# A decoder layer on one core: low parts of the projections' weights by an adding transfer in place of a subtraction

## The chip, the cores and the metric

The kernel runs on one core of a Trainium2 chip. The core has five engines that run their own instruction lists side by side: TensorE (PE, matmuls, with its weight loads as PEld), VectorE (DVE), ScalarE (ACT), GpSimd (POOL) and SyncE (SP, which here only issues transfers). Transfers between the chip's memory and the core's own memory run on 16 transfer engines; SyncE, ScalarE and GpSimd can issue them. The metric is the device time of one execution in microseconds; times are given as the median of some runs.

## What is computed

One layer with two token mixers, a merge, and a feed-forward part, in float32, for 512 tokens of width 1024:

```python
proj = x @ w_in                                     # 1024 x 8720, the projections
q, k, v, z, b_raw, a_raw, lru_x, lru_g, gate_dn, gate_lru = split(proj)
qkv  = silu(causal_depthwise_conv([q, k, v], dn_conv_w))
o    = gated_delta_rule_chunked(l2(q), l2(k), v, g, beta)
y_dn = (rms(o) * dn_norm_w * silu(z)) @ w_branch_dn
h    = rg_lru(causal_depthwise_conv(lru_x, lru_conv_w) + lru_conv_b, ...)
y_lru = (h * gelu(lru_g)) @ w_branch_lru
merged = sigmoid(gate_dn + b) * y_dn + sigmoid(gate_lru + b) * y_lru
h = layer_norm(alpha * x + merged @ w_out)
h = layer_norm(alpha * h + (silu(h @ w_gate) * (h @ w_up)) @ w_down)
```

## The kernel before

Every large product is made of three matmuls in a reduced float32 format: both operands are split into a high part, rounded to that format, and a low part, the remainder. `mm3` (line 154) issues high x high, high x low and low x high (lines 155, 156, 157), so line 157 is the one that reads the low part of the weights.

A weight block is 128 columns of a matrix: a tile of 128 partitions by 8 row groups by 128 columns, 512 KB, read in rows of 512 bytes. `load_w` (line 164) has SyncE fetch it into `wr` (3 buffers). `split_w` (line 173) makes the high part `wh` and the low part `wl` (3 buffers each, pool `wp`): `split_flat` (line 133) has ScalarE round the block into `wh` (line 135) and then subtracts `wh` from `wr` into `wl` (line 121), on VectorE in one piece or, where it is told `G`, on GpSimd in two halves of 512 columns.

`columns` (line 404) turns a matrix's columns into jobs of one block: fetch and split, then 8 x 3 matmuls of 512 tokens into one PSUM bank, then a function that takes the result on (conv, gate, SiLU). `play` (line 303) keeps the block in work and two more fetched ahead. All projections (`dn_proj`, `z_proj`, `lru_pair`, `gate_pair`) run through `columns` with `G`, in an order written in line 20: 64 blocks, called block 0 to block 63 here in the order in which TensorE works on them, from about 43 to 509 us. Between the steps of a block `advance` lets small chains onto TensorE: the delta rule of each head pair (`dn_chain`) and the gates of each LRU pair (`lru_chain`), whose other work lies on VectorE, ScalarE and GpSimd (masks, copies, clears). TensorE's list is ordered by hand from a table of latencies (line 23); the other engines' lists are ordered by a scheduler at build time, each engine then runs its list strictly in order.

The first FFN pair (line 1090) is split ahead of its use into tiles `f0h` and `f0l` of its own, also with `G`: four blocks. The branch matrices, `w_out` and the rest of the FFN are split with VectorE's subtraction; the change leaves them as they are.

Of the kernel before, what the change touches and what calls it, by code (L numbers as in the profile page):

```python
# [11 lines left out]
AF = mybir.ActivationFunctionType  # L12
ALU = mybir.AluOpType
# [20 lines left out]
P = 128  # L34
T = 512
D = 1024
NK = D // P
# [4 lines left out]
CQ, CK, CV, CZ, CB, CA = 0, 1024, 2048, 3072, 4096, 4104  # L42
# [4 lines left out]
def layer_kernel(  # L47
# [9 lines left out]
    V, S, G, PE = nc.vector, nc.scalar, nc.gpsimd, nc.tensor  # L57
# [13 lines left out]
    def slot(name, dt=F32):  # L71
        if not line:
            raise RuntimeError(f"no slot for {name}")
        tag = line.pop(0)
        t = big.tile([P, 2, T], dt, tag=tag, name=name)
        held[id(t)] = (t, tag)
        return t
# [12 lines left out]
    def bankp(name):  # L90
        return bank("p", name)
# [4 lines left out]
    def urgent():  # L96

        return tc.high_priority(offset=500)
# [12 lines left out]
    def f(ap):  # L111
        return ap.bitcast(F32)

    def flat(t):
        return t.rearrange("p a b -> p (a b)")
# [4 lines left out]
    def tt(eng, o, a, b, op):  # L120
        return eng.tensor_tensor(out=o, in0=a, in1=b, op=op)  # L121
# [4 lines left out]
    def act(o, i, func, **kw):  # L126
        return S.activation(out=o, in_=i, func=func, **kw)  # L127
# [5 lines left out]
    def split_flat(hi, lo, src, eng=None):  # L133

        S.copy(out=hi, in_=src)  # L135
        n = src.shape[1]
        step = 512 if eng is G else n
        for c in range(0, n, step):
            tt(eng or V, lo[:, c:c + step], src[:, c:c + step], f(hi[:, c:c + step]), ALU.subtract)
# [14 lines left out]
    def mm3(ps, wh, wl, rh, rl, start, stop):  # L154
        PE.matmul(ps, wh, rh, start=start, stop=False)  # L155
        PE.matmul(ps, wh, rl, start=False, stop=False)  # L156
        PE.matmul(ps, wl, rh, start=False, stop=stop)  # L157
# [3 lines left out]
    def view_w(t, a, b):  # L161
        return t[:, :a * b].rearrange("p (a b) -> p a b", a=a)

    def load_w(src, raw=None):

        wcount[0] += 1
        if raw is None:
            raw = wp.tile([P, 1024], F32, tag="wr", bufs=3, name=f"wr{wcount[0]}")
        v = view_w(raw, *src.shape[1:])
        nc.sync.dma_start(out=v, in_=src)  # L170
        return v

    def split_w(raw, eng=None, hi=None, lo=None):

        wcount[0] += 1
        if hi is None:
            hi = wp.tile([P, 1024], F32R, tag="wh", name=f"wh{wcount[0]}")
        if lo is None:
            lo = wp.tile([P, 1024], F32R, tag="wl", name=f"wl{wcount[0]}")
        n = raw.shape[1] * raw.shape[2]  # L180
        split_flat(hi[:, :n], lo[:, :n], raw.rearrange("p a b -> p (a b)"), eng)
        return view_w(hi, *raw.shape[1:]), view_w(lo, *raw.shape[1:])

    def rows(w):
        return w.rearrange("(kt p) c -> p kt c", p=P)

    win = rows(w_in[0])
# [51 lines left out]
    xT = []  # L239
# [23 lines left out]
    with tc.manual_schedule(engines={mybir.EngineType.Activation, mybir.EngineType.DVE}):  # L263
        for k in range(NK):
            transpose_x(k)
            if k == 1:
                n = NK * 16
# [22 lines left out]
    def advance(flush=False):  # L290
        while flush and chains:
            clock[0] += 0.68
            advance()
        for ch in list(chains):
            while ch in chains and ch[0] <= clock[0]:
                try:
                    pe, lat = next(ch[1])
                    ch[0] = clock[0] + pe + lat
                    clock[0] += pe
                except StopIteration:  # L300
                    chains.remove(ch)
# [19 lines left out]
    def start(gen, lat):  # L321
        chains.append([clock[0] + lat, gen])
# [71 lines left out]
    for b in range(4):  # L394
        G.tensor_copy(out=eye32[32 * b:32 * b + 32],
                      in_=ident[32 * b:32 * b + 32, 32 * b:32 * b + 32])
# [4 lines left out]
    V.tensor_reduce(out=up, in_=eye32[:, 0:16], axis=AX.X, op=ALU.add)  # L401
    V.tensor_reduce(out=low, in_=eye32[:, 16:32], axis=AX.X, op=ALU.add)

    def columns(src, rhs, name, then, eng=None, nk=NK):

        def job(j):
            def fetch():
                return split_w(load_w(src[:, :, j * P:j * P + P]), eng)

            def use(wh, wl):  # L410
                ps = bankp(f"{name}_{j}")
                for k in range(nk):
                    mm3(ps, wh[:, k], wl[:, k], rhs[k][:, 0], rhs[k][:, 1], k == 0, k == nk - 1)
                    if k < nk - 1:
                        yield
                then(j, ps)
                yield
            return fetch, use

        for j in range(src.shape[2] // P):  # L420
            yield job(j)

    def conv(o, ps, w, n, **kw):
        with urgent():
            act(o, ps, AF.Identity, scale=w(3, n), **kw)
            for d in (1, 2, 3):
                stt(o[:, d:], ps[:, :T - d], w(3 - d, n), o[:, d:], ALU.mult, ALU.add)
# [15 lines left out]
    def dn_proj(col, p):  # L443
        t = qkv[col, p] = slot(f"x{col}_{p}")

        def then(j, ps):
            conv(t[:, j], ps, qkv_w, col // P + 2 * p + j)
            act(t[:, j], t[:, j], AF.Silu)
            if j == 1:
                done[f"{col}_{p}"] = clock[0] + LAT["conv"]  # L450

        if col == CK:
            start(dn_chain(p), 0.0)
        if p == 0 and col != CV:
            for j in range(2):
                then(j, first[(0 if col == CK else 2) + j])
        else:
            c = col + 256 * p
            yield from columns(win[:, :, c:c + 256], xT, f"pj{col}_{p}", then, G)

    sz = [None] * 4

    def z_proj(p):
        sz[p] = slot(f"sz{p}")

        def then(j, ps):
            with urgent():
                act(sz[p][:, j], ps, AF.Silu)
            if j == 1:
                done[f"{CZ}_{p}"] = clock[0]  # L470

        c = CZ + 256 * p
        yield from columns(win[:, :, c:c + 256], xT, f"pj{CZ}_{p}", then, G)

    def dn_chain(p):

# [295 lines left out]
    def lru_pair(p):  # L772
        n0 = 2 * p
        u, r, ig = slot(f"u{p}"), slot(f"r{p}"), slot(f"ig{p}")
        gw = wg.tile([P, 4, P], F32, tag="gr" if p % 2 else "gs", name=f"gr{p}")
        nc.sync.dma_start(out=gw[:, 0:2], in_=lru_w_a[0, n0:n0 + 2].rearrange("n i o -> i n o"))
        nc.sync.dma_start(out=gw[:, 2:4], in_=lru_w_i[0, n0:n0 + 2].rearrange("n i o -> i n o"))

        def then_u(j, ps):
            conv(u[:, j], ps, lru_w, n0 + j, bias=lru_p(0, n0 + j))  # L780
            if j == 1:
                start(lru_chain(p, u, r, ig, gw), LAT["u"])

        keep = []

        def then_g(j, ps):
            keep.append(ps)
            if j == 1:
                while p not in gls:
                    clock[0] += 0.68  # L790
                    advance()
                with urgent():
                    for i in range(2):
                        act(gls[p][:, i], keep[i], AF.Gelu_apprx_tanh)
                done[f"gl{p}"] = clock[0]

        c = CLX + 256 * p
        yield from columns(win[:, :, c:c + 256], xT, f"lx{p}", then_u, G)
        c = CLG + 256 * p
        yield from columns(win[:, :, c:c + 256], xT, f"lg{p}", then_g, G)  # L800

    def lru_chain(p, u, r, ig, gw):
        n0 = 2 * p
# [33 lines left out]
    def gate_pair(col, p):  # L837
        g = slot(f"g{col}_{p}")

        def then(j, ps):  # L840
            with urgent():
                act(g[:, j], ps, AF.Sigmoid, bias=gate_b((0 if col == CGD else 8) + 2 * p + j))

        c = col + 256 * p
        yield from columns(win[:, :, c:c + 256], xT, f"g{col}_{p}", then, G)
        gates[p + (0 if col == CGD else 4)] = g

    def before_merge():
# [22 lines left out]
    for n in range(4 * NK):  # L871
# [7 lines left out]
        wh, wl = [t.rearrange("p (j k c) -> p j k c", j=2, k=2) for t in ws[k // 2]]  # L879
# [144 lines left out]
    for i in range(4):  # L1024
        t = slot(f"h1{i}")
# [16 lines left out]
    for m in range(4):  # L1042
        wh, wl = split_w(load_w(wo[:, 2 * m:2 * m + 2, 0:512]))
        for i in range(4):
            ts = slice(i * P, (i + 1) * P)
            for k in (2 * m, 2 * m + 1):
                mm3(pss[i], mT[k][:, 0, ts], mT[k][:, 1, ts], wh[:, k % 2], wl[:, k % 2], k == 0, k == NK - 1)
# [6 lines left out]
    for i in range(4):  # L1054
        ps = bankp(f"mx1_{i}")
        ts = slice(i * P, (i + 1) * P)
        for k in range(NK):
            if i > 1 and k == (5 if i == 2 else 3):
                transpose_h(i - 2)
            wh, wl = ws[k // 2]  # L1060
# [29 lines left out]
    for n, (src, then) in enumerate(ffn_pair(0)):  # L1090
        for j in range(2):
            tiles = [slot(f"f0{m}{n}{j}", F32R) for m in "hl"]
            wh, wl = split_w(load_w(src[:, :, j * P:j * P + P]), G, *[flat(t) for t in tiles])
            work.append((bankp(f"f0{n}{j}"), wh, wl, then, j, tiles))
    for half in range(2):
        ts = slice(256 * half, 256 * half + 256)
# [20 lines left out]
    for j in range(2):  # L1117
# [5 lines left out]
        for m in range(NF // 2):  # L1123
# [4 lines left out]
            for i in range(4):  # L1128
                ts = slice(i * P, (i + 1) * P)
                last = m == NF // 2 - 1  # L1130
                for c, ps in tops[i]:
                    n = ps.shape[1]
# [35 lines left out]
```

## Time and profile before

| | |
|---|---|
| median of 3 runs | 1030.63 us (1030.3 to 1031.08) |
| the profiled execution | 1029.83 us, of which the span of the profile is 1028.1 |
| TensorE busy | 999.7 us (97%), mean granted clock 0.995 |
| VectorE, ScalarE, GpSimd busy | 545.1, 425.5, 247.6 us |
| subtractions on GpSimd for the projections | 128, 172.4 us together |
| roundings of blocks on ScalarE | 145, 151.8 us together |
| transfers issued by SyncE for blocks of the projections | 64 of 512 KB, 3.7 us to land in the median |

A share of busy time is an average over stages; what a change is worth is read from the stage where it lies. In the rows, "wl<-wr,wh" is an operation that writes `wl` from `wr` and `wh`; the numbers of single buffers are left out. Rows of the timeline begin with the start (us from the span's start) and the duration (us), and end with the idle time of the engine ahead of the row and what ended it. A transfer's "issue" row is its time on the engine that issues it; "to landing" runs from issue to the landing of its data.

### The profile page before, as it was taken

What the parts mean: (1) busy time and instruction counts of PE and PEld (TensorE: products, weight loads), DVE (VectorE), ACT (ScalarE), POOL (GpSimd) and SP (SyncE); (2) the same over time, 40 slices, a digit from 0 to 9 for tenths busy, and PEclk for the clock granted to TensorE, in tenths of its full rate; (3) what the DMA queues carried; (4) which work ended last, traced back from release to release, by engine and by line L of the source; (5) the groups of instructions that cost most, each with busy time, mean ns of one, the idle gap of its engine ahead of it and who ended that gap; (6) DMA issues with size and microseconds to landing.
All of it is one profiled execution on the core that took longest, in us unless ns stands there. A gap on an engine that the chain in (4) does not pass through costs nothing. (4 is left out here: it accounts for less than half of the span.)

```text
span 1028.1 us, 14179 instructions
## 1 busy us (share of the span) xinstructions
PE 999.7 (97%) x5630; PEld 824.5 (80%) x5630; DVE 545.1 (53%) x1161; ACT 425.5 (41%) x576; POOL 247.6 (24%) x234
## 2 busy tenths in 40 slices
PE   7999989999999999999999999999999999999995
PEld 4887767877887888788888888898888888888885
DVE  3769989837777872264333556823333333312426
ACT  5589463368326643764321333323223322321222
POOL 2372624516332723274100003000000000000006
PEclk9999999999999999999999999999999999999998
DMA  8332223223222323154334337003333433333222
GB/s 252 106 101 54 80 73 84 63 72 82 63 62 73 87 63 93 47 142 115 102 94 153 103 115 213 1 23 101 103 95 110 123 103 88 97 103 100 85 62 82
DMA packets 150663, 96.79 MB, mean 94 GB/s; under 512 B 4476, under 2 KB 139837, under 8 KB 150597
## 3 DMA queue, kind: packets, MB, share of 16 engines
q1 hardware_dynamic: 148064, 91.52, 30.8%
q0 software_dynamic: 1216, 4.20, 1.2%
q8 instruction: 44, 0.72, 0.3%
q10 hardware_dynamic: 1316, 0.16, 0.1%
q14 instruction: 23, 0.18, 0.1%
HBM read 93.76 MB, written 2.11 MB: 93 GB/s over the span
## 5 line engine op out<-in xcount | busy, mean ns | idle before, releaser
L135 ACT CAST wh<-wr 128x1024 fp32r<-128x1024 f32 x145 | 151.8, 1048 | 410.5 <-issue 132.8
L121 POOL TENSOR_TENSOR wl<-wr,wh 128x512 fp32r<-128x512 f32 x128 | 172.4, 1369 | 216.5 <-ACT wh L135 207.0
L121 DVE TENSOR_TENSOR wl<-wr,wh 128x1024 fp32r<-128x1024 f32 x81 | 99.2, 1225 | 206.8 <-ACT wh L135 206.8
L155 PE MATMUL pj<-xT,wh 128*128 128x512 f32 x224 | 92.5, 413 | 0.0
L156 PE MATMUL pj<-xT,wh 128*128 128x512 f32 x224 | 88.2, 394 | 0.0
L157 PE MATMUL pj<-xT,wl 128*128 128x512 f32 x224 | 88.2, 394 | 0.0
L127 ACT ACT_TABLE_LOAD x62 | 79.5, 1283 | 12.3 <-DMA rw<-in_lru_conv_w 6.8
L156 PE MATMUL dn<-wl,fT 128*128 128x512 f32 (+1 forms) x168 | 63.3, 377 | 0.0
L155 PE MATMUL dn<-wh,fT 128*128 128x512 f32 (+1 forms) x168 | 63.3, 377 | 0.0
L157 PE MATMUL dn<-wh,fT 128*128 128x512 f32 (+1 forms) x168 | 63.2, 376 | 0.0
L156 PE MATMUL fg<-hk,wh 128*128 128x512 f32 x160 | 62.3, 389 | 0.0
L155 PE MATMUL fg<-hk,wh 128*128 128x512 f32 x160 | 62.3, 389 | 0.0
L157 PE MATMUL fg<-hk,wl 128*128 128x512 f32 x160 | 62.2, 389 | 0.0
L155 PE MATMUL fu<-hk,wh 128*128 128x512 f32 x160 | 62.2, 389 | 0.0
L156 PE MATMUL fu<-hk,wh 128*128 128x512 f32 x160 | 62.2, 389 | 0.0
L157 PE MATMUL fu<-hk,wl 128*128 128x512 f32 x160 | 62.2, 389 | 0.0
L121 POOL TENSOR_TENSOR h<-h,g 128x512 f32<-128x512 f32 x6 | 8.1, 1358 | 193.2 <-ACT h L127 193.2
L155 PE MATMUL g<-xT,wh 128*128 128x512 f32 x128 | 51.1, 399 | 0.0
L157 PE MATMUL g<-xT,wl 128*128 128x512 f32 x128 | 50.0, 391 | 0.0
L157 PEld LDWEIGHTS pj<-xT,wl 128*128 128x128 f32 x224 | 42.5, 190 | 9.3
L156 PE MATMUL g<-xT,wh 128*128 128x512 f32 x128 | 49.9, 390 | 0.0
L124 DVE SCALAR_TENSOR_TENSOR x<-pj,cols,x 128x511 f32<-128x511 f32 (+2 forms) x60 | 44.5, 742 | 9.9 <-ACT x L127 9.5
(358 smaller groups left out, 2241.6 us busy)
## 6 DMA issues: line engine op xcount, KB each, us to landing
wr<-in_w_in SPq DMA_DIRECT2D x64, 512.0 KB, 3.7
wr<-in_w_ffn_gate SPq DMA_DIRECT2D x22, 512.0 KB, 3.7
wr<-in_w_ffn_up SPq DMA_DIRECT2D x22, 512.0 KB, 3.6
wr<-in_w_ffn_down SPq DMA_DIRECT2D x22, 512.0 KB, 3.7
wr<-in_w_branch_lru SPq DMA_DIRECT2D x8, 512.0 KB, 3.6
wr<-in_w_branch_dn SPq DMA_DIRECT2D x8, 512.0 KB, 4.0
wr<-in_w_out SPq DMA_DIRECT2D x8, 512.0 KB, 4.2
wk<-in_w_in SPq DMA_DIRECT2D x8, 256.0 KB, 6.1
```

What stands on the lines that cost most here:

```text
L121: return eng.tensor_tensor(out=o, in0=a, in1=b, op=op)
L124: return V.scalar_tensor_tensor(out=o, in0=a, scalar=s, in1=b, op0=op0, op1=op1)
L127: return S.activation(out=o, in_=i, func=func, **kw)
L135: S.copy(out=hi, in_=src)
L155: PE.matmul(ps, wh, rh, start=start, stop=False)
L156: PE.matmul(ps, wh, rl, start=False, stop=False)
L157: PE.matmul(ps, wl, rh, start=False, stop=stop)
```

## The change

For the projections and the first FFN pair the low part is no longer subtracted by GpSimd. ScalarE writes the negated block into `wl` (rounded to the same format as the high part), and GpSimd issues a second transfer of the same block from the chip's memory, which adds what it reads to what lies in `wl`. ScalarE also rounds the block into `wh`, as before. The fetch into `wr` by SyncE stays.

```diff
-    def split_w(raw, eng=None, hi=None, lo=None):
+    def split_w(raw, src=None, hi=None, lo=None):
...
-        split_flat(hi[:, :n], lo[:, :n], raw.rearrange("p a b -> p (a b)"), eng)
-        return view_w(hi, *raw.shape[1:]), view_w(lo, *raw.shape[1:])
+        flat_raw = raw.rearrange("p a b -> p (a b)")
+        h, l = view_w(hi, *raw.shape[1:]), view_w(lo, *raw.shape[1:])
+        if src is None:
+            split_flat(hi[:, :n], lo[:, :n], flat_raw)
+        else:
+            act(lo[:, :n], flat_raw, AF.Copy, scale=-1.0)
+            G.dma_start(out=l, in_=src, accum_op=ALU.add)
+            S.copy(out=hi[:, :n], in_=flat_raw)
+        return h, l
...
-    def columns(src, rhs, name, then, eng=None, nk=NK):
+    def columns(src, rhs, name, then, by_dma=False, nk=NK):
...
-                return split_w(load_w(src[:, :, j * P:j * P + P]), eng)
+                cols_j = src[:, :, j * P:j * P + P]
+                return split_w(load_w(cols_j), cols_j if by_dma else None)
...
-            wh, wl = split_w(load_w(src[:, :, j * P:j * P + P]), G, *[flat(t) for t in tiles])
+            cols_j = src[:, :, j * P:j * P + P]
+            wh, wl = split_w(load_w(cols_j), cols_j, *[flat(t) for t in tiles])
```

The calls of `columns` in `dn_proj`, `z_proj`, `lru_pair` and `gate_pair` pass `True` where they passed `G`. TensorE's and SyncE's lists keep their instructions in the same order. GpSimd's list has one transfer where two subtractions stood; ScalarE's list has 68 more instructions, and the scheduler orders it anew in places.

ScalarE ahead of block 8, beside the first LRU pair (`r`, `ig`, `a` are the LRU's gates, `gl` its GELU, `x_0` a conv's output; `wh_903`, `wl_904` belong to block 8). Before:

```order
L127 ACTIVATE ig_441<-lw_1_1_842,cols 128x512
L127 ACTIVATE r_440<-r_440,c_231 128x512
L127 ACT_TABLE_LOAD
L127 ACTIVATE a_868<-r_440,c8n 128x512
L135 CAST wh_903<-wr_901 128x1024
L127 ACTIVATE x_0_651<-pj_0_0_908,cols 128x512
```

The same place now:

```order
L127 ACTIVATE ig_441<-lw_1_1_842,cols 128x512
L127 ACTIVATE r_440<-r_440,c_231 128x512
L127 ACT_TABLE_LOAD
L127 ACTIVATE a_868<-r_440,c8n 128x512
L127 ACTIVATE wl_904<-wr_901 128x1024
L127 ACTIVATE x_0_651<-pj_0_0_908,cols 128x512
L127 ACTIVATE r_440<-r_440,c_231 128x512
L127 ACTIVATE ig_441<-a_868 128x1024
L189 CAST wh_903<-wr_901 128x1024
```

The negation stands where the rounding stood, and the rounding comes three instructions later. A little above this place block 7's negation (`wl_779`) now stands between the first GELU and the gates.

ScalarE for block 9 (`wh_981`, `wl_982`; `xa` is a square for a norm). Before:

```order
L127 ACTIVATE xa_916<-kt_0_921 128x512
L127 ACTIVATE xa_916<-kt_1_929 128x512
L135 CAST wh_981<-wr_979 128x1024
L127 ACT_TABLE_LOAD
L127 ACTIVATE ig_441<-ig_441,tiny 128x1024
L127 ACTIVATE x_0_651<-pj_0_1_986,cols 128x512
```

The same place now:

```order
L127 ACTIVATE xa_916<-kt_0_921 128x512
L127 ACT_TABLE_LOAD
L127 ACTIVATE ig_441<-ig_441,tiny 128x1024
L127 ACTIVATE x_0_651<-pj_0_1_986,cols 128x512
L127 ACTIVATE xa_916<-kt_1_929 128x512
L127 ACT_TABLE_LOAD
L127 ACTIVATE x_0_651<-x_0_651 128x512
L127 ACTIVATE wl_982<-wr_979 128x1024
L189 CAST wh_981<-wr_979 128x1024
```

The block's first instruction on ScalarE has moved behind two table loads, the square root, a conv's first step and a SiLU.

GpSimd for blocks 7 and 8 (`Fl`, `F` are decay masks, `xa` and `Yf` the delta rule's tiles). Before:

```order
L514 AFFINE_SELECT Fl_1061<-F_1060 128x1024
L516 AFFINE_SELECT F_1060<-F_1060 128x1024
L121 TENSOR_TENSOR wl_779<-wr_776,wh_778 128x512
L593 COPY xa_562<-Fl_457 32x256 x4
L121 TENSOR_TENSOR wl_779<-wr_776,wh_778 128x512
L605 MEMSET xa_562 128x8x16
L121 TENSOR_TENSOR wl_904<-wr_901,wh_903 128x512 x2
```

The same place now:

```order
L602 COPY xa_562<-Fl_457 32x256 x4
L525 AFFINE_SELECT F_754<-F_754 128x1024
L614 MEMSET xa_562 128x8x16
L188 DMA wl_779<-in_w_in 128x8x128
L188 DMA wl_904<-in_w_in 128x8x128
L625 MEMSET Yf_1682 128x1024
```

One transfer stands in the place of two subtractions, and the third head pair's masks (`F_1060`) have moved behind these blocks.

## Rows read from the trace of the kernel before

**Rows 1.** The page, part 1: busy time by engine

```profile
PE 999.7 (97%) x5630; PEld 824.5 (80%) x5630; DVE 545.1 (53%) x1161; ACT 425.5 (41%) x576; POOL 247.6 (24%) x234
```

**Rows 2.** TensorE's waits; line, waited for: us, times, longest us

```profile
PE i L669 <- DVE xa L664: 2.3, 2, 1.4
...
PE m L633 <- DVE xa L627: 0.6, 1, 0.6
```

**Rows 3.** Stretches: length, busy (x count) by engine, TensorE's clock, transfer share, GB/s

```profile
0.00:25.00 25.00, 18.64 (x83) 11.97 (x83) 9.71 (x18) 12.78 (x23) 7.02 (x17) 1.00 0.86 259
100.00:150.00 50.00, 45.16 (x412) 34.76 (x411) 46.85 (x149) 26.59 (x34) 23.94 (x29) 1.00 0.30 80
```

**Rows 4.** Subtraction and rounding, 0 to 560 us: ns min/median/max, first and last start

```profile
L121 POOL TENSOR_TENSOR wl<-wr,wh x128: 1259/1289/2302, 32.3 to 493.8; 128x512 fp32r<-128x512 f32 x128
L135 ACT CAST wh<-wr x74: 1027/1048/1062, 31.2 to 554.7; 128x1024 fp32r<-128x1024 f32 x74
```

**Rows 5.** Transfers: GpSimd's time for an issue, landings of g and b, list of issues

```profile
L981 POOL DMA_DIRECT2D g<-in_ln_g x2: 561/561/561, 454.8 to 791.4; - x2
L227 POOL DMA_DIRECT2D nA<-in_dn_A_log x1: 704/704/704, 1.4 to 1.4; - x1
DMA to landing us min/median/max: 4.0/4.5/5.3
h<-in_x POOLq DMA_DIRECT2D x4, 512.0 KB, 6.2
wr<-in_w_in SPq DMA_DIRECT2D x64, 512.0 KB, 3.7
```

**Rows 6.** Timeline, block 61 in the dense stretch: rounding, first matmul on the low part

```profile
480.42 1.05 ACT L135 CAST wh<-wr 128x1024 fp32r<-128x1024 f32 x1 [3.80 <-issue]
491.73 0.39 PE L157 MATMUL g<-xT,wl 128*128 128x512 f32 x1
```

**Rows 7.** First FFN pair: subtractions and their use, first and last start

```profile
L121 POOL TENSOR_TENSOR f0l<-wr,f0h x8: 1282/1295/1301, 621.5 to 630.3; 128x512 fp32r<-128x512 f32 x8
L157 PE MATMUL f<-hk,f0l x64: 279/283/284, 652.4 to 679.0; 128*128 128x256 f32 x64
```

**Rows 8.** Timeline, blocks 2 and 16: rounding, first matmul on the low part

```profile
45.98 1.04 ACT L135 CAST wh<-wr 128x1024 fp32r<-128x1024 f32 x1
54.11 0.39 PE L157 MATMUL lx<-xT,wl 128*128 128x512 f32 x1
153.37 1.04 ACT L135 CAST wh<-wr 128x1024 fp32r<-128x1024 f32 x1
161.53 0.39 PE L157 MATMUL pj<-xT,wl 128*128 128x512 f32 x1
```

**Rows 9.** Timeline, blocks 8 and 9: rounding, a SiLU, first matmuls on low parts

```profile
92.84 1.04 ACT L135 CAST wh<-wr 128x1024 fp32r<-128x1024 f32 x1
96.97 0.39 PE L157 MATMUL pj<-xT,wl 128*128 128x512 f32 x1
102.28 0.64 ACT L127 ACTIVATE x<-x 128x512 f32<-128x512 f32 x1
104.21 0.39 PE L157 MATMUL pj<-xT,wl 128*128 128x512 f32 x1
```

**Rows 10.** Timeline, blocks 52 and 53 rounded, first matmul on 52's low part

```profile
435.52 1.98 ACT L135 CAST wh<-wr 128x1024 fp32r<-128x1024 f32 x2
438.10 0.48 PE L157 MATMUL g<-xT,wl 128*128 128x512 f32 x1
```

**Rows 11.** Timeline, VectorE's operations on two tiles beside a subtraction on GpSimd

```profile
306.30 0.23 DVE L121 TENSOR_TENSOR xa<-xa 128x80 f32<-128x80 f32 x1
307.18 2.54 POOL L121 TENSOR_TENSOR wl<-wr,wh 128x512 fp32r<-128x512 f32 x2 [7.91 <-ACT wh L135]
308.02 1.82 DVE L121 TENSOR_TENSOR xa<-xa 128x88 f32<-128x88 f32 x2
```

More of the change, by code (lines that the diff above doesn't have):

```diff
@@ L458, in dn_proj @@
             c = col + 256 * p
-            yield from columns(win[:, :, c:c + 256], xT, f"pj{col}_{p}", then, G)
+            yield from columns(win[:, :, c:c + 256], xT, f"pj{col}_{p}", then, True)
     sz = [None] * 4
@@ L472, in z_proj @@
         c = CZ + 256 * p
-        yield from columns(win[:, :, c:c + 256], xT, f"pj{CZ}_{p}", then, G)
+        yield from columns(win[:, :, c:c + 256], xT, f"pj{CZ}_{p}", then, True)
     def dn_chain(p):
@@ L797, in lru_pair @@
         c = CLX + 256 * p
-        yield from columns(win[:, :, c:c + 256], xT, f"lx{p}", then_u, G)
+        yield from columns(win[:, :, c:c + 256], xT, f"lx{p}", then_u, True)
         c = CLG + 256 * p
-        yield from columns(win[:, :, c:c + 256], xT, f"lg{p}", then_g, G)
+        yield from columns(win[:, :, c:c + 256], xT, f"lg{p}", then_g, True)
     def lru_chain(p, u, r, ig, gw):
@@ L844, in gate_pair @@
         c = col + 256 * p
-        yield from columns(win[:, :, c:c + 256], xT, f"g{col}_{p}", then, G)
+        yield from columns(win[:, :, c:c + 256], xT, f"g{col}_{p}", then, True)
         gates[p + (0 if col == CGD else 4)] = g
```

## The prediction

> **What bounds the kernel now.** I read the page's busy shares first: TensorE is busy for 999.7 of 1028.1 us, every other engine for about half or less [rows 1]. So the time is TensorE's list of matmuls plus its holes, and the edit touches neither list nor order. Second come TensorE's waits by cause: in the stage of the projections seven causes, all of them VectorE, from 2.3 us down to 0.6, 10.0 us together; no wait for a weight block stands in the list [rows 2]. The table by stretches says the same: of the 50 us from 100 on, TensorE is busy for 45.16 [rows 3]. So the change can win at most about 10 us there, and only through VectorE; it can lose without limit, by making a weight block late. What decides is how early each block is ready now, and how long the new path to a low part is.
>
> **The old path.** ScalarE rounds the block (1.05 us) as soon as TensorE frees the buffer, then GpSimd subtracts in two halves of 1.29 us: 64 blocks, 128 subtractions [rows 4]. From the end of the rounding a low part takes about 2.6 us.
>
> **The new path.** ScalarE writes the negated block (same shape, priced as the rounding: 1.05 us), GpSimd issues a transfer, and TensorE's third matmul of the block waits until it has landed. ScalarE gets 68 more instructions, 71 us, VectorE nothing, SyncE nothing. I call D the time from the end of the negation to the landing. No accumulating transfer is in the trace, so D is put together:
> - Issue. GpSimd's transfers of 128 rows take 0.56 us on its engine, and one whose rows are 32 bytes takes 0.70, so the time isn't set by bytes [rows 5]. A block has 8 x 128 = 1024 rows of 512 bytes. If the 0.56 is fixed, the issue costs 0.56; if it grows with the rows, 8 x 0.56 = 4.5; if the second operand adds half as many, 6.7. I take 2.5, midway between the first two, since the two row kinds shown have the same count and can't tell fixed from growing.
> - Moving. In the first 25 us the transfer engines are 0.86 busy at 259 GB/s [rows 3], so 512 KB (0.524 MB) take 0.524/301 GB/s = 1.74 us. The sum needs the old contents read as well: 1.74 if that is free, 3.5 if it costs as much as the read from memory. I take 3.5.
> - The rest. GpSimd's own 512 KB transfers land 4.0 to 5.3 us after issue in one group, 6.2 in the median of another; the queue of SyncE lands the same weight block in 3.7 [rows 5]. 4.5 less 0.56 less 1.74 leaves 2.2.
>
> D = 2.5 + 3.5 + 2.2 = 8.2 us; bounds 0.56 + 1.74 + 1.7 = 4.0 and 6.7 + 3.5 + 2.2 = 12.4. Against the old 2.6 that is 5.6 us later per block.
>
> On the second read the Trainium skill (Collectives: The Full Stack, "Why ReduceScatter is half of AllGather") says that an add in a transfer needs two source reads and so runs at about half the rate of a copy. It speaks against this change, and by it the 3.5 would stand. No row here shows such a transfer. With a free second read D would be 6.4, only blocks 8, 9 and 52 would be late, and the sum below would be about 10 us.
>
> **Where 8.2 us don't fit.** Three buffers hold blocks n to n+2. When TensorE ends block n, block n+3 may be written, and two blocks of matmuls pass before it is wanted. In the densest stretch the rounding starts at 480.42 and the low part is first wanted at 491.73 [rows 6]: 491.73 - 481.47 leaves 10.3 us for D. So 8.2 is hidden in the steady state, and the four FFN blocks have 20 us of cover (last subtraction at 630.3 + 1.3, first use at 652.4) [rows 7]. It isn't hidden where ScalarE reaches the block late, because the conv, gate and LRU work of the chains stands ahead of it. I add D to the end of the rounding there and compare with the first matmul that reads the low part:
> - Block 2: rounding ends 47.02, plus 8.2 and 0.1 for the handover is 55.3; wanted at 54.11 [rows 8]. Late by 1.2.
> - Block 8: the rounding starts at 92.84 (ScalarE is busy with the first LRU pair), the low part is wanted at 96.97 [rows 9]. In the new order of ScalarE block 7's negation also stands in that run: 93.88 + 1.05 + 8.3 = 103.2. Late by 6.2.
> - Block 9: its negation now stands behind the SiLU that ran at 102.28 (0.64 long) [rows 9], where its rounding stood before three table loads. With 1.05 for each of block 7's and 8's negations less block 9's rounding, it ends at about 105.1; plus 8.3 is 113.4 against 104.21 + 6.2 = 110.4. Late by 3.0 more.
> - Block 52, last LRU pair: two roundings from 435.52 on, the first ends 436.5; plus 8.3 is 444.8 against 438.10 [rows 10]. Late by 6.7.
> - Block 16: 153.37 + 1.04 + 8.3 = 162.7 against 161.53 [rows 8]: 1.1. Three more places read the same way (blocks 26, 38, 54) give 2.2 together.
>
> Sum 1.2 + 6.2 + 3.0 + 6.7 + 1.1 + 2.2 = 20.4 us.
>
> **What comes back.** VectorE's operations on two tiles stall while GpSimd subtracts: 0.23 us for one of 128x80, but 1.82 for two of 128x88 under the subtraction at 307.18 [rows 11]. The 128 subtractions go, so some of the 10.0 us of waits for VectorE [rows 2] go. Bounds 0 and 10; I take 3, because the long runs of small dependent operations in the chains remain, and ScalarE, which feeds them too, gets slower. GpSimd's engine time falls (172 us out, at most 300 in), but its queue stays in order: selects, copies and clears of the chains stand behind a transfer that waits for a negation, as they stood behind a subtraction that waited for a rounding. Nothing.
>
> Net 20.4 - 3 = 17.4. On the profiled execution's 1029.8 us that is 1047.2; the median of the runs shown lies 0.8 above that execution: **1048 us**.
>
> **The rivals.**
> 1. *The landing is nearly hidden.* With D at 4.0 to 5.7 only blocks 8 and 52 are late, by 2 to 5 us and by 2.5 to 4.2, and VectorE gives back up to 10: from -5 to +9, so 1026 to 1039. For it: GpSimd's plain transfers do land in 4.0. Against it: none of those has 1024 rows or a second operand. The Trainium skill (DMA: Bandwidth & Descriptors, "Anatomy of one DMA") gives 2.0 us plus bytes/436 GB/s, 3.2 us here, an estimate from that page; the rows show 4.0 to 7.0 for GpSimd's 512 KB, so the trace lies above it. By it the loss would be about 2 us and VectorE's gain would win.
> 2. *The path outgrows the buffers* (the far end of the slower side). The point is D = 10.3, the dense cover. At 10.2 (issue 4.5) the eight places lose 2 us more each, 16, and some six new ones about 1 each, 7: 20.4 + 16 + 7 - 3 = 40, so 1071. At 12.4 each turn of the three buffers is 2.1 us too long as well: 64/3 x 2.1 = 45 beside the 40, so 1116. For it: 1024 rows are eight times what any GpSimd transfer here issues. Against it: SyncE's queue moves the same 1024 rows in 3.7. The Trainium skill (SBUF — State Buffer, the box on "DVE blocks DMA") says that certain VectorE operations keep GpSimd from writing the descriptors of its transfers; no row here shows that, and it would push this way.
> 3. *ScalarE becomes the bound.* 71 us more on an engine busy for 425 of 1028 in all. It runs full only beside the LRU pairs, five times, and blocks 8 and 9 above carry that price. At worst two more microseconds at each of the five: 10 more, 1058. That lies in the forecast's own range.
> 4. *The transfer doesn't do what it says*, and the program falls back on more, smaller transfers: same direction as rival 2.
>
> **How the numbers follow.** A measurement here can tell about 0.2%, 2 us. Forecast with rival 3 (D from 6 to 10, 1034 to 1070): 0.52, all slower. Rival 2 with 4: 0.22, all slower, a quarter of it above 1112. Rival 1: 0.26, of which 0.15 is faster, 0.09 within 0.2%, 0.02 slower. Together faster 0.15, same 0.09, slower 0.76. The range leaves out the best part of rival 1 below 1027 and the top of rival 2 above 1112.
>
> **What would show it.** Right: TensorE's waits name the low part's transfer, longest at blocks 8, 9 and 52, none in the dense stretch after 460; a GpSimd transfer takes 2 to 3 us on its engine and lands about 8 after issue; VectorE's busy time falls by some tens of us. Wrong: landings under 6 us (rival 1); a wait at every block (rival 2); TensorE waiting for ScalarE with the transfers long landed (rival 3). If VectorE's relief is worth 10 and D is below 6, the sign is wrong.

## The result and the profile after

The changed kernel takes 1067.19 us (median of 4 runs, 1065.84 to 1067.64) where the kernel before took 1030.67 beside it: a ratio of 1.0352, 95% interval 1.0334 to 1.037. It is slower by 36.5 us; the forecast said slower by 17.4, less than half of that. The span of the profiled execution is 1064.1 us against 1028.1 of before, 36.0 more; where these went is the question of this part.

The page after, part 1 (busy time by engine) and from part 2 the clock that TensorE was granted and the share of the transfer engines, in 40 slices:

```profile
PE 1008.7 (95%) x5630; PEld 829.6 (78%) x5630; DVE 504.6 (47%) x1161; ACT 492.8 (46%) x646; POOL 168.6 (16%) x166
...
PEclk9989999999999999989999999799999999999998
DMA  8695996975788879799933439402333433333222
```

Against [rows 1] VectorE lost 40.5 us, GpSimd 79.0, and ScalarE gained 67.3. TensorE, with the same 5630 matmuls, is busy for 9.0 us more, and idle for 55.4 in place of 28.4: the span's 36.0 are 27.0 us of waiting and 9.0 of slower work.

TensorE's waits after (line, waited for: us in total, times, longest us):

```profile
PE pj L157 <- DMA wl<-in_w_in: 12.2, 5, 3.6
PE hp L1046 <- DVE h L124: 10.5, 1, 10.5
PE g L157 <- DMA wl<-in_w_in: 7.6, 2, 6.6
PE lx L157 <- ACT F L127: 6.2, 1, 6.2
...
PE i L669 <- DVE vb L121: 1.3, 1, 1.3
```

Of the seven waits for VectorE in [rows 2] one is left, 1.3 us. In their place stand waits for the low part's transfer (12.2 and 7.6, and the 6.2 of `lx`, which is block 2: the profile names an operation of ScalarE that ended at 61.31 us, but the matmul reads the low part, which landed at 61.29, and starts at 61.42), together 26.0 us, and one that no row of before hinted at: 10.5 us of the transposes `hp` for the norm's result `h`, between the projections and the FFN.

The low part's transfers after: GpSimd's time for an issue (min/median/max in ns) and the time to landing, then the medians of the list of issues (GpSimd's and SyncE's queue, us to landing), then the two queues (packets, MB, share of 16 engines' span):

```profile
L188 POOL DMA_DIRECT2D wl<-in_w_in x64: 1534/1550/1642, 34.3 to 519.4; - x64
...
DMA to landing us min/median/max: 6.7/7.6/12.1
```

```profile
q1 hardware_dynamic: 148064, 91.52, 30.2%
q0 software_dynamic: 71936, 39.86, 29.2%
...
wr<-in_w_in SPq DMA_DIRECT2D x64, 512.0 KB, 4.8
wl<-in_w_in POOLq DMA_DIRECT2D x64, 512.0 KB, 7.6
```

With 0.4 us from the negation's end to the issue, D is 0.4 + 7.6 = 8.0 us; the prediction had 8.2. So the size of the new operation was right, and the miss lies in what it meets. The issue took 1.55 us, less than the 2.5 taken, and the way from there more.

The next table is worked out from the timelines of the two kernels: how much later than before TensorE reaches the first matmul on the low part of a block, and at which blocks it fell back or caught up by over 1 us.

| block | 2 | 3 | 8 | 9 | 11 | 14 | 17 | 19 | 26 | 27 | 28 | 29 | 36 | 40 | 52 | 53 | 63 |
|---|---|---|---|---|---|---|---|---|---|---|---|---|---|---|---|---|---|
| step, us | +6.6 | +2.0 | +4.0 | +3.8 | -1.6 | -3.9 | +2.5 | -2.1 | +1.2 | -2.2 | +3.5 | +1.7 | -1.6 | +1.1 | +6.8 | +1.9 | 0 |
| late in all, us | 7.3 | 9.3 | 12.8 | 16.6 | 15.1 | 11.3 | 14.0 | 11.9 | 13.1 | 10.9 | 14.5 | 16.2 | 14.7 | 15.8 | 22.7 | 24.6 | 25.0 |

All steps back, those below 1 us with them, are 36.8 us, all steps forward 11.8: the projections end 25.0 late. The last 11.0 us of the 36.0 come behind them, at the wait of `hp` and the slower matmuls after it. Not every step is a late block: at 3, 29 and 53 TensorE doesn't wait (block 3's low part landed at 66.08 us and is read at 69.75); their 5.6 us are slower matmuls behind the waits of blocks 2, 28 and 52.

Each long wait also slows the work behind it. Stretches around block 52 (length, then busy time and count of PE, PEld, DVE, ACT and POOL, the granted clock, the transfer share, GB/s):

```profile
444.00:454.00 10.00, 10.00 (x47) 8.09 (x46) 2.88 (x3) 9.92 (x13) 1.14 (x1) 1.00 0.01 2
454.00:461.00 7.00, 0.38 (x2) 0.15 (x1) 4.85 (x5) 6.96 (x8) 1.96 (x2) 0.78 0.93 151
461.00:465.00 4.00, 4.00 (x10) 3.15 (x11) 0.00 (x0) 0.67 (x1) 1.55 (x1) 0.53 1.01 183
465.00:469.00 4.00, 4.00 (x21) 3.35 (x21) 0.61 (x2) 0.54 (x1) 0.00 (x0) 1.00 1.33 199
```

TensorE works at 1.00 (2.4 GHz), waits 6.6 us for the low part, and when it goes on it is granted 0.53, nearly the lower level of 1.2 GHz: 10 matmuls in 4 us in place of 21. Such stretches stand behind the other long waits too (the first two 8s and the 7 in the clock's row are the slices of block 2, block 52 and `hp`), and the best version below, without long waits, is busy for 998.9 us. So I read the 9.0 us of busy time as theirs; the prediction's sum had no such term.

### The profile page after: what moved, and what is told of

Same layout as the page of the kernel before. It is cut to its first block, busy times and chain, and to the rows that moved or that the text cites. A ratio compares the mean times of both kernels' runs of the same rounds, so it can differ in the third digit from the quotient of the medians.

```text
span 1064.1 us, 14197 instructions
## 1 busy us (share of the span) xinstructions
PE 1008.7 (95%) x5630; PEld 829.6 (78%) x5630; DVE 504.6 (47%) x1161; ACT 492.8 (46%) x646; POOL 168.6 (16%) x166
## 3 DMA queue, kind: packets, MB, share of 16 engines
q0 software_dynamic: 71936, 39.86, 29.2%
## 4 chain that ended last, share of the span: by engine, by line
PE 78%; DMA 9%; issue 4%; ACT 4%; DVE 3%; POOL 1%; SPq 0%; DVEq 0%; ACTq 0%; POOLq 0%
DMA wl<-in_w_in 5%; PE dn L156 4%; PE dn L157 4%; PE dn L155 4%; PE fu L157 3%; PE fg L157 3%; PE fg L155 3%; PE fu L155 3%; PE fg L156 3%; PE fu L156 3%; PE pj L155 3%; PE pj L157 3%; PE pj L156 3%; PE g L157 2%; PE g L155 2%
## 5 line engine op out<-in xcount | busy, mean ns | idle before, releaser
L188 POOL DMA_DIRECT2D wl<-in_w_in x64 | 99.3, 1552 | 311.3 <-ACT wl L127 238.3
L157 PE MATMUL pj<-xT,wl 128*128 128x512 f32 x224 | 89.7, 400 | 12.4 <-DMA wl<-in_w_in 12.2
L127 ACT ACTIVATE wl<-wr 128x1024 fp32r<-128x1024 f32 x64 | 67.1, 1049 | 0.0
L124 DVE SCALAR_TENSOR_TENSOR x<-pj,cols,x 128x511 f32<-128x511 f32 (+2 forms) x60 | 44.5, 742 | 16.2 <-ACT x L127 15.7
L155 PE MATMUL g<-xT,wh 128*128 128x512 f32 x128 | 51.9, 405 | 0.0
```

Of the source, the lines that this page charges most:

```text
L124: return V.scalar_tensor_tensor(out=o, in0=a, scalar=s, in1=b, op0=op0, op1=op1)
L188: G.dma_start(out=l, in_=src, accum_op=ALU.add)
```

## The experiments

Times are medians beside runs of the kernel before on the same chip (1030.6 to 1031.1 us). "Late" is against the kernel before, at TensorE's matmuls.

### The two losses are apart

The four blocks of the first FFN pair go back to GpSimd's subtraction; the projections stay as changed. (Here and below, "..." in a diff stands for lines that hand `eng` or a count of the blocks through.)

```diff
...
-            wh, wl = split_w(load_w(cols_j), cols_j, *[flat(t) for t in tiles])
+            wh, wl = split_w(load_w(cols_j), None, *[flat(t) for t in tiles], eng=G)
```

> The changed kernel, with the first FFN pair's four low parts again subtracted by GpSimd; the projections keep the adding transfer. Theory A (the pair's four adding transfers fill the transfer engines from 647 to 672 us, SyncE's next blocks land late, and VectorE's subtractions of those blocks stand ahead of the first norm): the 10.5 us wait of the transposes goes, 1067.2 - 11 = 1056, in 1054 to 1058. Rival (the wait comes from arriving late, or from ScalarE's list): 1064 to 1068.

Measured: 1057.4 us, ratio 1.0256 [1.0235, 1.0277]. The wait of `hp` is 0.5 us there; the waits for the projections' low parts are as long as in the kernel after (14.0, 7.4 and 5.7). So some 10 us belong to four transfers.

The opposite: the kernel before with the transfer in the FFN pair alone.

> The kernel before, with the adding transfer in the first FFN pair alone. Theory A: 1030.7 + 11 = 1042, in 1039 to 1044, and the transposes wait about 10 us for VectorE. Rival (the four blocks have 20 us of cover, as the prediction had it): 1029 to 1033.

Measured: 1041.34 us, ratio 1.0103 [1.0086, 1.012]; `hp` waits 11.7 us. Four transfers cost 10.6 us by themselves, the 64 of the projections the other 26.

### What the four FFN transfers hold up

In the prediction these four had 20 us of cover. The kernel after, its ScalarE, from the last of the pair's negations to the norm's square root:

```profile
652.61 1.06 ACT L127 ACTIVATE f0l<-wr 128x1024 fp32r<-128x1024 f32 x1 [1.04 <-DMA wr<-in_w_ffn_up]
...
660.45 1.05 ACT L135 CAST wh<-wr 128x1024 fp32r<-128x1024 f32 x1 [5.83 <-DMA wr<-in_w_ffn_gate]
665.68 1.05 ACT L135 CAST wh<-wr 128x1024 fp32r<-128x1024 f32 x1 [4.18 <-DMA wr<-in_w_ffn_gate]
670.83 1.04 ACT L135 CAST wh<-wr 128x1024 fp32r<-128x1024 f32 x1 [4.10 <-DMA wr<-in_w_ffn_up]
671.89 1.28 ACT L127 ACT_TABLE_LOAD   x1
676.24 0.20 ACT L127 ACTIVATE ln_rs<-ln_rs 128x1 f32<-128x1 f32 x1 [3.07 <-DVE ln_rs L1013]
```

and TensorE's first transposes behind it:

```profile
678.09 1.97 PE L1046 MATMUL hp<-ident,h 128*128 128x128 f32 x8 [10.46 <-DVE h L124]
```

The square root of the norm (`ln_rs`) stands in ScalarE's list behind the roundings of the next three weight blocks, and each of those waits for its load. VectorE's subtractions of the same blocks stand ahead of the norm in the same way (at 661.53, 666.76 and 671.90). The loads are SyncE's ordinary ones, and they are late because the adding transfers lie on the same transfer engines. From the list of issues in 645 to 665 us of the kernel after, us to landing in the median:

```profile
wr<-in_w_ffn_up SPq DMA_DIRECT2D x4, 512.0 KB, 16.1
f0l<-in_w_ffn_gate POOLq DMA_DIRECT2D x2, 512.0 KB, 10.8
wr<-in_w_ffn_gate SPq DMA_DIRECT2D x2, 512.0 KB, 14.0
f0l<-in_w_ffn_up POOLq DMA_DIRECT2D x2, 512.0 KB, 17.1
```

and in 645 to 670 us of the run with the pair subtracted:

```profile
wr<-in_w_ffn_gate SPq DMA_DIRECT2D x6, 512.0 KB, 3.5
wr<-in_w_ffn_up SPq DMA_DIRECT2D x4, 512.0 KB, 3.7
```

3.5 us became 14 to 16. First I took VectorE's subtractions for what holds the norm, and gave the next pair's to GpSimd (the rest as in the kernel after):

```diff
...
-            yield from columns(sg, hk, f"fg{p}", then_g)
-            yield from columns(su, hk, f"fu{p}", then_u)
+            yield from columns(sg, hk, f"fg{p}", then_g, eng=G if p == 1 else None)
+            yield from columns(su, hk, f"fu{p}", then_u, eng=G if p == 1 else None)
```

> The changed kernel, with the four FFN blocks that follow the first pair subtracted by GpSimd in place of VectorE; the pair itself keeps its adding transfers. Theory A (the late blocks hold up the norm only because their subtractions stand ahead of it in VectorE's list): the 10.5 us wait of the transposes goes though those blocks land as late as now, 1055 to 1059. Rival (the pair's own low parts, or the transfer engines, are what is late): 1064 to 1068.

Measured: 1064.04 us, ratio 1.0331 [1.0312, 1.035]. The theory fell: at most 3 us came back (the interval overlaps that of the kernel after), not 8 to 12. VectorE is free in that trace, and waits 11.78 us for ScalarE instead, where the same three roundings wait for the same loads:

```profile
672.21 1.04 ACT L135 CAST wh<-wr 128x1024 fp32r<-128x1024 f32 x1 [4.20 <-DMA wr<-in_w_ffn_up]
673.27 1.28 ACT L127 ACT_TABLE_LOAD   x1
674.56 0.20 ACT L127 ACTIVATE ln_rs<-ln_rs 128x1 f32<-128x1 f32 x1
```

So ScalarE's list is enough to hold the norm, with VectorE's out of the way; what stays in both runs are the late loads. The last test of them comes below, with two transfers in the place of four.

### What the landing costs, and what ScalarE

The same program with a plain copy in place of the adding transfer; it leaves out the addition, so its low parts are the block itself and not the remainder.

```diff
-            G.dma_start(out=l, in_=src, accum_op=ALU.add)
+            G.dma_start(out=l, in_=src)
```

> The changed kernel with GpSimd's transfer as a plain copy: it overwrites the negated block in place of adding to it, so the low parts are not those of the reference; everything else stays, negations included. Theory A (the path to the low part is too long): issue 1.55 as now, landing 1.55 + 1.74 + 1.7 = 5 us after issue in place of 7.6, the projections lose 7 to 12 in place of 25, the FFN pair 2 to 5 in place of 11: 1040 to 1048. Rival B (ScalarE's 71 us and its list): 1060 to 1067.

Measured: 1044.67 us, ratio 1.0131 [1.011, 1.0152]. GpSimd's issue and the landing, and its queue:

```profile
L188 POOL DMA_DIRECT2D wl<-in_w_in x64: 873/873/922, 35.1 to 502.2; - x64
...
DMA to landing us min/median/max: 4.2/5.3/7.6
```

```profile
q0 software_dynamic: 71936, 39.86, 19.5%
```

The projections are 0.1 us late at block 51 and 7.7 at the end (steps back 18.9, steps forward 11.2), and `hp` waits 7.0 us. The add itself makes the landing 2.3 us later and the time 22.5 us longer.

The reverse: ScalarE's negation stays in place, ahead of each rounding, but GpSimd subtracts as in the kernel before, and no second transfer is made. The FFN pair is as in the kernel before, so there are 64 negations.

```diff
...
-            G.dma_start(out=l, in_=src, accum_op=ALU.add)
-            S.copy(out=hi[:, :n], in_=flat_raw)
+            split_flat(hi[:, :n], lo[:, :n], flat_raw, G)
```

> The changed kernel with GpSimd's subtraction in place of its transfer, and the negations of ScalarE kept, whose result the subtraction overwrites: ScalarE has the 68 more instructions, no added transfer runs. Theory A: ScalarE's load by itself costs little, 1031 to 1038. Rival B (ScalarE's load and list are the cause): 1048 or more.

Measured: 1044.94 us, ratio 1.0132 [1.0113, 1.0152], between the two expectations. TensorE is 14.1 us late at the end of the projections with no second transfer at all: 62 us more on ScalarE (487.5 busy against 425.5), in its strict order, cost 14 us. By the two timelines 5.8 us of that are waiting (the largest in the projections are 3.7 and 2.4 us for VectorE, 2.3 and 2.0 before, and 1.8 for ScalarE) and 8.4 slower matmuls; the stretch that [rows 3] shows at a granted clock of 1.00 is at 0.92 here:

```profile
100.00:150.00 50.00, 43.80 (x379) 33.49 (x378) 42.83 (x114) 35.42 (x45) 29.24 (x31) 0.92 0.31 85
```

So the transfer isn't the whole loss, and ScalarE, which the prediction gave at most 10 us on top in a rival, is a large part of it.

### The negation's place in ScalarE's list

Nothing is taken away here: the negation alone is marked with the priority that the program already uses elsewhere (`urgent`), so the scheduler puts it as early in ScalarE's list as the raw block and the buffer allow.

```diff
-            act(lo[:, :n], flat_raw, AF.Copy, scale=-1.0)
+            with urgent():
+                act(lo[:, :n], flat_raw, AF.Copy, scale=-1.0)
```

> The changed kernel with the negations given precedence in ScalarE's list: block 8's stands five instructions earlier, block 9's nine. Theory A (blocks are late because ScalarE reaches their negation late and 8 us of path follow): the late places at blocks 8, 9, 17, 28, 52 shrink by 3 to 5 us each, the projections end 10 to 18 late in place of 25: 1050 to 1060. Rival C (doubled traffic on the transfer engines is what delays, wherever the negation stands): 1064 to 1070.

Measured: 1042.64 us, ratio 1.0108 [1.0093, 1.0124], better than either theory. GpSimd's issue and landing are as in the kernel after:

```profile
L189 POOL DMA_DIRECT2D wl<-in_w_in x64: 1524/1545/1642, 34.1 to 495.9; - x64
...
DMA to landing us min/median/max: 6.6/7.5/10.6
```

and the projections end 1.4 us late, not 25.0. Block 52 shows how. The kernel after, negation of block 52 on ScalarE and its first matmul on the low part:

```profile
449.90 0.71 ACT L127 ACTIVATE r<-r,c 128x512 f32<-128x512 f32 x1
450.51 1.05 ACT L127 ACTIVATE ig<-a 128x1024 f32<-128x1024 f32 x1
451.46 1.05 ACT L127 ACTIVATE wl<-wr 128x1024 fp32r<-128x1024 f32 x1
...
460.85 0.80 PE L157 MATMUL g<-xT,wl 128*128 128x512 f32 x1 [6.62 <-DMA wl<-in_w_in]
```

The buffer had been free since 440.2 (the end of block 49's matmuls); for 11 us ScalarE worked on the LRU gates. With the early negation, where the buffer is free at 423.0:

```profile
424.31 0.60 ACT L127 ACTIVATE gl<-lg 128x512 f32<-128x512 f32 x1
424.80 1.05 ACT L127 ACTIVATE wl<-wr 128x1024 fp32r<-128x1024 f32 x1
```

From that negation's start to TensorE's first use of the low part at 437.60 it is 12.8 us, and the 1.05 of the negation and D fit in. So at this block an 8 us landing costs almost nothing; what cost was the landing behind a negation that the scheduler had left where a rounding with a 2.6 us path had been harmless. Over the whole stage the 1.4 us are a balance: the steps back are still 14.8 us, 7.7 of them by block 4, and the steps forward 13.4.

What is left in the trace of that run:

```profile
PE hp L1047 <- DVE h L124: 11.3, 1, 11.3
...
PE lx L157 <- DMA wl<-in_w_in: 2.5, 1, 2.5
PE pj L157 <- DMA wl<-in_w_in: 2.2, 2, 1.3
```

The wait of `hp` stands untouched, and together with the first experiment that gives the sum: the two remedies in one kernel.

> The two remedies together: every negation of the 64 blocks of the projections stands as early in ScalarE's list as its raw block allows, and the FFN pair's low parts come from GpSimd's subtraction, as in the kernel before. Theory (two separate losses, the negation's place in ScalarE's list, 24 us, and the FFN pair's transfers, 11 us): the first remedy alone gave 1042.6 with a wait of 11.3 us for the norm left in its trace, the second alone took 9.8 off, so 1031 to 1034, the time of the kernel before within 0.3%. Rival (the landing's 8.1 us costs something by itself wherever the block stands, and ScalarE's extra 1.05 us a block too): 1036 or more, with the projections' end late by 5 us or more.

Measured: 1032.02 us, ratio 1.0005 [0.9995, 1.0016]: 10.6 us less, the time of the kernel before. The two losses add up. (It is a balance again: 8.4 us late at block 4, 1.3 at the end of the projections.) With two of the pair's four blocks by transfer (against the kernel just shown):

```diff
-            wh, wl = split_w(load_w(cols_j), None, *[flat(t) for t in tiles], eng=G)
+            wh, wl = split_w(load_w(cols_j), cols_j if n == 0 else None, *[flat(t) for t in tiles],
+                             eng=G if n else None)
```

> The early negations stay; of the FFN pair's four blocks the two of the gate come by the adding transfer, the two of the up weights by GpSimd's subtraction. With all four by transfer the time was 1042.6. Theory (the three loads that follow share the transfer engines with the adding transfers ahead of them, some 3.5 to 4.4 us for each transfer, and the norm's square root stands behind these loads' roundings on ScalarE): two transfers in the place of four take about half of the 11 us away, 1035 to 1038. Rival (it is the negations, or the f0 blocks' own late landing, that hold the transposes): no more than 2 us better than 1042.6.

Measured: 1035.38 us, ratio 1.004 [1.0027, 1.0052]; `hp` waits 3.3 us. Four, two and no transfers give 1042.6, 1035.4 and 1032.0, in line with loads that queue behind the adding transfers.

### The first blocks, and where it pays

The first place of the table is block 2, where the prediction had 1.2 us late and the trace 6.6. ScalarE in the kernel after, in front of block 2's negation:

```profile
48.89 0.22 ACT L127 ACTIVATE egl<-F 128x8 f32<-128x8 f32 x1 [6.07 <-DMA F<-gd]
...
53.00 1.04 ACT L127 ACTIVATE wl<-wr 128x1024 fp32r<-128x1024 f32 x1
```

and the same operation in the kernel before:

```profile
42.82 0.22 ACT L127 ACTIVATE egl<-F 128x8 f32<-128x8 f32 x1 [0.52 <-DMA F<-gd]
```

`egl` waits for a broadcast of the decay rows that SyncE issues, and at that time the adding transfers of blocks 0 and 1 are on the transfer engines. The negation of block 2 stands behind it. If that is the cause, blocks 0 and 1 by subtraction should take it away (the rest as in the kernel after):

```diff
...
-                return split_w(load_w(cols_j), cols_j if by_dma else None)
+                if not by_dma:
+                    return split_w(load_w(cols_j))
+                pcount[0] += 1
+                n = pcount[0] - 1
+                add = n > 1
+                return split_w(load_w(cols_j), cols_j if add else None, eng=None if add else G)
```

> The changed kernel with blocks 0 and 1 subtracted by GpSimd. Theory: block 2's 6.6 us (1.2 forecast) come from the adding transfers of blocks 0 and 1, which slow the broadcast of the decay rows, for which ScalarE waits ahead of block 2. Then that wait ends near 43 us in place of 48.9, block 3 is 1 to 4 late in place of 9.3, and the end gains 3 to 7: 1060 to 1064. Rival (ScalarE's new list alone): no change, 1066 to 1068.

Measured: 1070.31 us (1063.24 to 1072.73), ratio 1.0372 [1.034, 1.0404]: nothing gained. In its trace `egl` waits 0.30 us, so the cause was named rightly, and block 2 is 3.4 us late in place of 7.3. But blocks 3 and 4, now the second and third transfer, fall back by 3.2 and 1.6 (TensorE is 8.2 us late at block 4, 9.3 in the kernel after), and blocks 17 and 18 by 7.4 in place of 2.5. The loss moved on to the next blocks.

Transfer only for blocks whose low part lay ready more than 5.6 us ahead of its use in the kernel before (11, 12, 14, 15, 19 to 25, 27 to 34, 36, 37; 21 of the 64, where the expectation says 23 and half, and not all blocks with such a lead), without the mark on the negation, all others and the FFN pair by subtraction:

> The adding transfer only for 23 blocks of the projections with a lead of over 5.6 us before (11, 12, 14, 15, 19 to 25, 27 to 34, 36, 37), GpSimd's subtraction for the others and for the first FFN pair. Theory A: these have room for the longer path, so nothing is late, and VectorE is relieved of half the subtractions beside it: 1026 to 1031. Rival C (traffic) or B (ScalarE's load): 1034 or more.

Measured: 1029.04 us, ratio 0.9987 [0.9975, 0.9998], as expected and just below the kernel before. Finally the early negations with blocks 0 to 4 and the FFN pair subtracted:

```diff
...
+                add = n > 4
...
+            with urgent():
+                act(lo[:, :n], flat_raw, AF.Copy, scale=-1.0)
```

> Early negations; blocks 0 to 4 of the projections and the FFN pair are subtracted by GpSimd as in the kernel before, blocks 5 to 63 come by the adding transfer. In the run with early negations alone TensorE fell back 7.7 us by block 4, where the decay rows' broadcasts cross with the adding transfers, gained 9.2 us from block 10 to 36 (the waits for VectorE that GpSimd's subtraction had lengthened), and lost 3 us at blocks 16, 18 and 56. Theory: without the first five the fall of 7.7 us is spared, of which the gains of 3.9 at block 14 may partly have been its recovery, so 1024 to 1030. Rival (the early fall was slack that comes back by itself, or blocks 5 to 8 now take its place): 1031 to 1035.

Measured: 1021.54 us (1020.55 to 1021.85), ratio 0.9902 [0.9886, 0.9919]. This version beats both kernels, by 9.5 us and by 45.6. Its page and TensorE's waits in the projections:

```profile
PE 998.9 (98%) x5630; PEld 823.8 (81%) x5630; DVE 507.6 (50%) x1161; ACT 483.3 (47%) x637; POOL 176.0 (17%) x175
...
PE m L650 <- DVE Fl L124: 0.7, 1, 0.7
PE pj L157 <- DMA wl<-in_w_in: 0.4, 1, 0.4
```

TensorE is ahead of the kernel before by 10.3 us at block 36, at the very places where the kernel after had caught up (blocks 11, 14, 19, 27 and 36). That these are the waits for VectorE that GpSimd's subtraction lengthens, and not a gift of the early place on ScalarE, is for the last run to tell: the kernel before with its roundings, not negations, marked in the same way.

```diff
-        S.copy(out=hi, in_=src)
+        if eng is G:
+            with urgent():
+                S.copy(out=hi, in_=src)
+        else:
+            S.copy(out=hi, in_=src)
```

> The kernel before (all blocks subtracted by GpSimd), with the rounding of each block that GpSimd subtracts put as early in ScalarE's list as the negation stood in the runs with early negations; no transfer, no negation. It is the control to the run of 1021.5. Theory (what that run gained are the waits for VectorE that GpSimd's subtraction lengthens, some 10 us, which only the transfer takes away): the subtractions and the waits stay, so 1028 to 1034. Rival (the early place on ScalarE's list is what pays, whoever makes the low part): 1019 to 1025, with the path in the projections ahead by 6 us or more at block 36.

Measured: 1031.12 us, ratio 1.0005 [0.9994, 1.0016]. Of the 10.0 us of waits for VectorE 7.5 stay, among them:

```profile
PE m L637 <- DVE Fl L124: 2.4, 1, 2.4
...
PE ks L712 <- DVE Fl L729: 1.3, 1, 1.3
PE ks L712 <- DVE Fl L124: 1.3, 1, 1.3
PE i L673 <- DVE xa L668: 1.2, 2, 0.9
```

At block 36 this kernel is 0.8 us ahead, where the run with transfers was 10.3. One of that run's five places is a gift of the early place after all: at block 27 the control gains the same 3.6 us, but it loses 2.4 at block 11, where the other gains 0.9. So in the sum the early place alone pays nothing; the transfer in place of the subtraction is worth about 10 us, as soon as its own path is started early enough.

## Why the prediction was right in sign and wrong in size

- **D, right.** 8.2 us forecast, 8.0 measured. Of its terms the issue was too high (2.5 against 1.55) and the way from the issue's end to the landing too low (5.7 against 6.05, the median landing of 7.6 less the issue).
- **Hidden in the dense stretch, right.** After block 53 TensorE loses 0.4 us in ten blocks. The D of 10.3 from which rival 2 decides wasn't reached in the median (single blocks came to 12.4).
- **The late blocks, right in kind, short in the sum.** Block 52 was forecast at 6.7 and measured at 6.8, blocks 8 and 9 at 9.2 together and measured at 7.7. Block 2 was forecast at 1.2 and measured at 6.6: the step took its negation at the time of the old rounding, though ScalarE's list there waits for a transfer of SyncE that the new transfers delay. Of blocks 16, 26, 38 and 54 only 26 was late by more than 0.3 (1.2), and blocks 17, 28 and 40, with 7.2 us, were not in the list. They were not found because the sum set D against the times of before: block 28's negation ran at 267.21 us, 22.7 later than its rounding before, with TensorE only 10.9 late until there. The waits for low parts are 26.0 us where the sum had 20.4; the steps back, with the slower matmuls behind these waits, are 36.8.
- **What VectorE gives back, too small.** I took 3 out of 0 to 10; the waits for VectorE fell by 8.7 us, from 10.0 to 1.3, and the steps forward are 11.8. That this error of 5.7 nearly cancels the 5.6 by which the late blocks were short is luck. The row with two stalled tiles [rows 11] was nearer to the truth than my reason against it.
- **The FFN pair, the step that failed.** "20 us of cover" [rows 7] was measured on the pair's own use, and there it held. But the transfers were costed at nothing for others: SyncE's next loads landed after 14 to 16 us in place of 3.5, three roundings and three subtractions waited for them, and the norm stood behind both. The wait of `hp` is 10.5 us, with what follows it 11.0, over half of the 18.6 by which the span outgrew the forecast of 17.4.
- **The granted clock, missing.** 9.0 us of the loss are matmuls that ran longer, at a lower clock behind long waits, about 7.4 in the projections and 1.7 behind `hp`; the sum put them at nothing. They lie within the steps of the table and the 11.0, not beside them: a late block costs its wait and some more.
- **Rival 3, underrated.** ScalarE's 62 us cost 14 us by themselves in the run with negations and subtractions, where "at worst two more microseconds at each of the five" stood.
- **Rival 1, a wrong reading.** It calls only blocks 8 and 52 late. By the sum's own way block 9 comes 2.9 us behind block 8 whatever D is; with the plain copy, whose landing is 5.3, block 9 waited 4.2 us.

By the measured steps: 36.8 - 11.8 + 11.0 = 36.0, the span's 36.0. By cause: 26.0 of waits for low parts, less 8.7 of waits for VectorE, 10.5 for `hp`, 9.0 of slower matmuls, and 0.8 less of small waits elsewhere.

The Trainium skill (Collectives: The Full Stack, "Why ReduceScatter is half of AllGather") says of a ReduceScatter that its add needs two source reads, and that it runs at half the rate of a copy. The trace goes the same way but less far: on GpSimd's queue a packet took 0.292 x 16 x 1064.1 us / 71936 = 69 ns with the add and 0.195 x 16 x 1043.1 us / 71936 = 45 ns without, 1.5 times as long.

The Trainium skill (SBUF — State Buffer, the box on "DVE blocks DMA") says that VectorE can keep GpSimd from writing the descriptors of its transfers. No run here shows it: with VectorE busy for 504.6 of 1064.1 us, the 64 issues lie between 1.53 and 1.64 us.

## What to carry to other kernels

An operation that takes longer to arrive must also start earlier: look for the last instruction of its old path on every in-order list, see how long its input and its buffer had been ready by then, and move that start before judging the operation. A new transfer has a price for all transfers that are in flight beside it, so ask which load, issued by whom, lands later, and what stands behind the instruction that waits for it; its own cover says nothing of that. And a contended engine pays back at all its waits together, once the new path is out of the way.

## What the runs showed of the hardware that I had not expected

- GpSimd's issue of 1024 rows takes 0.87 us for a plain copy and 1.55 with an add, against 0.56 for 128 rows [rows 5]: eight times the rows cost 0.31 us more, the add 0.68.
- Four adding transfers in a row slow the loads beside them: landings of SyncE's 512 KB go from 3.5 to 14 to 16 us there; in the projections, where they come singly, only from 3.7 [rows 5] to 4.8.
- After a wait of 6.6 us TensorE was granted 0.53 for the next 4 us and 1.00 from then on; after the 10.5 us of `hp` 0.50 in the first 4 us and 0.84 in the next.
